# Layer 0's output weights split early, kept in DRAM and loaded ready-made

## The chip, the core and the metric

The kernel runs on one core of a Trainium2 chip. The core has five engines that each take their own instructions strictly in order and meet only at semaphores: TensorE (PE, matrix products and transposes into PSUM), VectorE (DVE), ScalarE (ACT), GpSimd (POOL) and SyncE (SP). In this kernel SP computes nothing; it issues the DMA transfers between DRAM and the on-chip memory SBUF, also in order. The metric is the device time of one execution in microseconds, the median of several runs.

## What is computed

Two encoder layers over 1024 tokens of width 1024. Layer 0 has a banded attention (A), a dense attention (B) and a cross-attention into 256 memory tokens (X); layer 1 has a differential attention and a cross-attention. In both, the heads' outputs are joined, gated and sent through one output matrix `w_out`:

```python
def even_layer(x, mem_n, table, norm_g, w_in, sink, q_norm, k_norm, w_mem_kv, w_out):
    h = rmsnorm(x, norm_g)
    aq, ak, av, bq, bk, bv, xq, gate = _split(h @ w_in, EVEN_SPLITS)
    y_a = windowed_gqa_sink(heads(aq, A_HEADS), heads(ak, A_KV_HEADS), heads(av, A_KV_HEADS), sink, table)
    qb = apply_axial_rope(rmsnorm(heads(bq, B_HEADS), q_norm), cos, sin)
    kb = apply_axial_rope(rmsnorm(heads(bk, B_KV_HEADS), k_norm), cos, sin)
    y_b = dense_gqa_blocked(qb, kb, heads(bv, B_KV_HEADS))
    y_x = memory_cross_attention(heads(xq, X_HEADS), mem_n, w_mem_kv)
    y = jnp.concatenate([y_a, y_b, y_x], axis=-1) * jax.nn.silu(gate)
    return x + y @ w_out
```

The kernel computes float32 products with operands of a reduced format (`fp32r`): each operand is split into a high part, `hi = fp32r(x)`, and a low part, `lo = fp32r(x - hi)`, and a product is the sum of three, hi·hi + hi·lo + lo·hi. So every weight tile needs a cast (the high part) and a subtraction (the low part) before PE can use it.

## The kernel before, in words

**Steps.** The attention of a layer is a list of steps; `run_steps` walks through it. Layer 0 has 8 steps of cross-attention (`NX = 8`), then 8 of the first dense head, then 64 in which dense and banded heads alternate by the string `PAT`. In the iteration of a dense step, PE computes the scores (`sb`, L511); DVE takes their minimum (`mn`), ACT the exponential (`mr` and `e`, L1068), DVE the reciprocal of the sum (`rz`) and POOL multiplies (`e`, L1072). One iteration later SP sends the result through a transfer, `er<-e` (`word_copy`, 512 KB; it copies the words into a tile of the other type). Three iterations after the scores PE transposes it (`te`, L542) in two PSUM banks, and ACT and DVE take the banks apart into `PTh` (L316) and `PTl` (L317). Every second step PE multiplies these with the values (`ob`, L1085). A banded step has the same shape with `sa`, `ta`, `PTa` and `oa`.

**Filling.** Between these, `Jobs` feeds PE with matmuls of other work, 8 at a time: the projections of the layer (`acc<-h,wh` and `acc<-h,wl`, L298) and, at the end of the list, the first part of the output projection (`pre`, L664, jobs made by `pre_jobs`). A projection job's weights are loaded into `wr` (two buffers), and split into `wh` and `wl` by DVE and POOL, when the job before it starts.

**Output weights.** `w_out` of a layer is 1024 x 1024, used as two halves of columns (`nh`) with 8 pieces of 128 rows (`k`) each. Its high and low parts go into tiles with the tag `h`, which hold the layer's normalized input until the last projection job, `last_gates`, has used it; the first half can be filled once that job's first half is done (`half_done`). From then on `wout_hook` calls `load_wout` for one piece at each call, twice in each step: a load of 256 KB into `wor` (a buffer `wr`, or a buffer `sg` for odd pieces), a cast on ACT into `woh` (L258) and a subtraction into `wol` (L259), on DVE for even pieces and on POOL for odd ones. A job `pre` may start when the 8 pieces of its half have been asked for.

**Order.** The program is written step by step, but the order on each engine is made by a scheduler that moves instructions between neighbouring steps by its own estimates. What runs is that order, engine by engine; a DMA, too, waits in SP's order for whatever it needs, with all transfers behind it.

## Time and profile before

| | us |
|---|---|
| median of 3 runs (1239.6 to 1243.0) | 1241.22 |
| the profiled execution's own time | 1242.6 |
| its span in the profile | 1240.8 |

The profile is that of one execution. Its page gives the busy time of each engine, the span in slices, the chain of work that ended last, and groups of like instructions. A row of a group reads: line, engine, operation, out<-in with its shapes, count, then busy time and mean duration of one, then the idle time of the engine in front of it with what ended it. A row of the timeline reads: start, duration, engine, line, operation, operands and count, and in brackets how long the engine stood idle before it and for whom. "issue" there means that the profile shows no one that was waited for. Matmuls overlap, so that the distance of their starts, not their duration, tells the pace.

### The profile page before, as it was taken

The numbers are of one execution on the slowest core, as the hardware profiler recorded it, in microseconds if no ns is written. First come the engines' busy times: TensorE is split into PE (matmuls) and PEld (weight loads), VectorE is DVE, ScalarE is ACT, GpSimd is POOL, SyncE is SP. The second block draws the span as 40 slices with busy tenths as digits, with TensorE's granted clock in tenths as the row PEclk, the third lists the DMA queues.
The fourth block names the chain that finished last, engine by engine and source line by source line (L and its number), as shares of the span: only waits on it lengthen the run. The fifth ranks groups of instructions, "written<-read, shape, count | busy, mean of one in ns | idle before, by whom it ended". The sixth has DMA issues, their size and how long they took to land. (4 is left out here: it accounts for less than half of the span.)

```text
span 1240.8 us, 19673 instructions
## 1 busy us (share of the span) xinstructions
PE 1204.3 (97%) x6806; PEld 1003.4 (81%) x6806; DVE 808.4 (65%) x1479; ACT 651.7 (53%) x1453; POOL 411.3 (33%) x390
## 2 busy tenths in 40 slices
PE   6999999999999999999999999999999999999997
PEld 4788888888887778887888788888787878887886
DVE  5547665477778778647355866766767676668544
ACT  6248754367667766533157733544544454456322
POOL 5023365466666655403122221222222121223100
PEclk9999999999999999999999999999999999999999
DMA  6654445545465565375645333243342432546364
GB/s 255 194 195 146 161 170 165 165 158 202 176 229 200 204 227 196 148 213 193 192 161 157 124 108 120 94 143 102 111 134 77 138 116 102 162 140 204 118 198 146
DMA packets 96638, 199.91 MB, mean 161 GB/s; under 512 B 11510, under 2 KB 31222, under 8 KB 96540
## 3 DMA queue, kind: packets, MB, share of 16 engines
q1 hardware_dynamic: 96540, 198.66, 47.8%
q8 instruction: 54, 0.88, 0.3%
q14 instruction: 44, 0.36, 0.1%
HBM read 79.32 MB, written 31.47 MB: 89 GB/s over the span
## 5 line engine op out<-in xcount | busy, mean ns | idle before, releaser
L298 PE MATMUL acc<-h,wh 128*128 128x512 f32 x1536 | 498.8, 398 | 1.6 <-DVE wh L240 0.6
L298 PEld LDWEIGHTS acc<-h,wh 128*128 128x128 f32 x1536 | 283.0, 188 | 66.3 <-issue 12.2
L298 PE MATMUL acc<-h,wl 128*128 128x512 f32 x768 | 304.7, 397 | 1.6 <-POOL wl L242 1.6
L242 POOL TENSOR_TENSOR wl<-wr,wh 128x512 fp32r<-128x512 f32 x96 | 124.1, 1294 | 335.7 <-DVE wh L240 146.7
L317 DVE TENSOR_TENSOR PTl<-te,PTh 128x512 fp32r<-128x512 f32 x224 | 148.5, 687 | 119.9 <-ACT PTh L316 117.3
L1466 ACT ACTIVATE e<-e,mn 128x1024 f32<-128x1024 f32 x96 | 110.2, 1149 | 125.9 <-DVE mn L1463 125.8
L298 PEld LDWEIGHTS acc<-h,wl 128*128 128x128 f32 x768 | 144.5, 188 | 35.2 <-issue 4.7
L316 ACT CAST PTh<-te 128x512 fp32r<-128x512 f32 x224 | 125.1, 590 | 18.5 <-PE te L542 15.2
L1463 DVE CUSTOM_DVE_ANT_0 e<-sc,toep 128x1024 f32<-128x1024 f32 x96 | 114.0, 1217 | 6.0 <-PE sc L1457 5.8
L1072 POOL TENSOR_TENSOR e<-e,rz 128x1024 f32<-128x1024 f32 x48 | 92.4, 1928 | 74.1 <-DVE rz L1071 56.9
L542 PEld LDWEIGHTS te<-identr,er 128*128 128x128 f32 x896 | 92.1, 143 | 17.5 <-issue 3.7
L542 PE MATMUL te<-identr,er 128*128 128x128 f32 x896 | 99.1, 245 | 4.9 <-issue 2.5
L240 DVE CAST wh<-wr 128x512 fp32r<-128x512 f32 x112 | 58.7, 526 | 38.2 <-PE acc L298 17.8
L1475 DVE SCALAR_TENSOR_TENSOR e<-e,mr 128x1024 f32<-128x1024 f32 x48 | 76.3, 1589 | 1.3
L1490 PE MATMUL oc<-PTh,v 128*128 128x256 f32 x384 | 74.8, 288 | 0.3 <-DVE ckl L1371 0.3
L664 PE MATMUL po<-woh,yh 128*128 128x512 f32 (+1 forms) x172 | 66.3, 385 | 0.0
L664 PE MATMUL po<-woh,yl 128*128 128x512 f32 (+1 forms) x172 | 66.1, 384 | 0.0
L664 PE MATMUL po<-wol,yh 128*128 128x512 f32 (+1 forms) x172 | 66.0, 384 | 0.0
L1063 DVE TENSOR_REDUCE mn<-sb 128x1 f32<-128x1024 f32 x48 | 58.4, 1217 | 7.2 <-PE sb L511 6.7
L1490 PEld LDWEIGHTS oc<-PTh,v 128*128 128x128 f32 x384 | 61.4, 191 | 0.7 <-DVE ckl L1371 0.6
L1068 ACT ACTIVATE e<-sb,mr,nrq 128x1024 f32<-128x1024 f32 x48 | 57.9, 1206 | 1.9
L319 ACT ACTIVATE yh<-yr 128x256 fp32r<-128x256 f32 (+2 forms) x56 | 24.0, 448 | 66.4 <-DMA yr<-ysc 33.8
(199 smaller groups left out, 2256.7 us busy)
## 6 DMA issues: line engine op xcount, KB each, us to landing
er<-e SPq DMA_DIRECT2D x112, 512.0 KB, 3.0
wr<-in_w_in SPq DMA_DIRECT2D x96, 256.0 KB, 2.7
ysc<-gy SPq DMA_DIRECT2D x16, 512.0 KB, 2.6
wor<-in_w_out SPq DMA_DIRECT2D x32, 256.0 KB, 3.3
cq<-sg SPq DMA_DIRECT2D x64, 128.0 KB, 2.9
ck<-sg SPq DMA_DIRECT2D x48, 128.0 KB, 2.3
er<-e SPq DMA_DIRECT2D x12, 384.5 KB, 2.9
xpsc<-xh SPq DMA_DIRECT2D x18, 256.0 KB, 2.4
```

The source lines that it names most:

```text
L240: nc.vector.tensor_copy(hi, raw)
L242: (nc.vector if fast else nc.gpsimd).tensor_tensor(out=lo, in0=raw, in1=hi, op=ALU.subtract)
L298: lastmm[0] = nc.tensor.matmul(acc, a, b[:, k, c0:c0 + n], start=(i == 0), stop=(i == 23))
L316: nc.scalar.copy(hi, src)
L317: return nc.vector.tensor_tensor(out=lo, in0=src, in1=hi, op=ALU.subtract)
L542: nc.tensor.transpose(to[:, i * P:(i + 1) * P], e[0][:, k * P:(k + 1) * P], idt)
L664: lastmm[0] = nc.tensor.matmul(acc, a, b, start=(start and n == 0), stop=(stop and n == 2))
L1072: nc.gpsimd.tensor_tensor(out=et, in0=et, in1=rz.to_broadcast([P, 1024]), op=ALU.mult)
L1463: nc.vector.tensor_tensor_reduce(out=et, in0=Sp, in1=toeps[h][:, w0:w0 + 1024], scale=1.0, scalar=BIG, op0=ALU.add, op1=ALU.min, accum_out ...
L1466: nc.scalar.activation(et, et, AF.Exp, bias=mn[:, m:m + 1], scale=-1.0, accum_out=z[:, m:m + 1])
L1475: nc.vector.scalar_tensor_tensor(out=es[0], in0=es[1], scalar=c, in1=es[0], op0=ALU.mult, op1=ALU.add)
L1490: nc.tensor.matmul(acc, V[:, kt, v, :], pt[:, kt, :], start=(n == 0), stop=(n == 23))
```

## The change

Layer 0's `w_out` is split earlier and in smaller pieces. From the step after the last of the cross-attention and one more (`i > NX`), each iteration of `run_steps` calls `early.step()`, until 32 pieces of 128 x 256 are done: it stores the two parts of the piece before into DRAM (`wo_d`, one tensor for each half and part), loads the next piece into half of a `wr` buffer, casts it on ACT and subtracts on POOL. The two results stand in a new pool `stage` with one buffer for each part.

`load_wout` then loads, for layer 0, the high and the low part from DRAM straight into the tiles `h`, 256 KB each, with no cast and no subtraction. Layer 1 stays as it was. A job `pre` with `k` pieces may now start when `k` pieces of its half have been asked for instead of 8, in both layers.

```diff
+    wo_d = [[[dr.tile([P, 8, 512], F32R, name="wo%d%d%s" % (l, nh, c)) for c in "hl"] for nh in range(2)]
+            for l in range(2)]
...
+    class Early:
+        def __init__(self, l, tiles):
+            self.l, self.n, self.tiles, self.held = l, 0, tiles, None
+
+        def store(self):
+            if self.held is not None:
+                hi, lo, nh, k, c = self.held
+                for d, t in zip(wo_d[self.l][nh], (hi, lo)):
+                    dma(d[:, k, c:c + 256], t)
+                self.held = None
+
+        def step(self):
+            self.store()
+            if self.n < 32:
+                i, c = divmod(self.n, 2)
+                nh, k = divmod(i, 8)
+                c = c * 256
+                self.n += 1
+                raw = wp.tile([P, 512], F32, tag="wr", name="wor", bufs=2)[:, 0:256]
+                dma(raw, w_out[self.l][KORD[self.l][k], :, nh * 512 + c:nh * 512 + c + 256])
+                hi, lo = self.tiles()
+                nc.scalar.copy(hi, raw)
+                nc.gpsimd.tensor_tensor(out=lo, in0=raw, in1=hi, op=ALU.subtract)
+                self.held = hi, lo, nh, k, c
...
     def load_wout(l, i, pl):
...
+        hi, lo = (t[:, k, :] for t in wtile[nh])
+        if l == 0:
+            for t, d in zip((hi, lo), wo_d[l][nh]):
+                dma(t, d[:, k, :])
+            return hi, lo
         raw = sg(M, "wor", F32) if i % 2 else wp.tile([P, 512], F32, tag="wr", name="wor", bufs=2)
         dma(raw, w_out[l][KORD[l][k], :, nh * 512:(nh + 1) * 512])
-        hi, lo = (t[:, k, :] for t in wtile[nh])
-        (nc.vector.tensor_copy if WHI[l] else nc.scalar.copy)(hi, raw)
+        nc.scalar.copy(hi, raw)
...
-                    when=lambda k=k, nhs=nhs: len(wout) >= 8 * nhs[-1] + 8 and all((l, m) in stored for m in range(k))))
+                    when=lambda k=k, nhs=nhs: len(wout) >= 8 * nhs[-1] + k and all((l, m) in stored for m in range(k))))
...
+    stage = pool(left, "stage", "left")
+    early = Early(0, lambda: [stage.tile([P, 256], F32R, tag="wo" + c, name="wo" + c, bufs=1) for c in "hl"])
...
+        if i > NX:
+            early.step()
```

Where instructions move, the scheduler's order shows it. First ACT in the middle of the alternating heads of layer 0 (about 319 us in the profile). Before (`yt` is the evacuation of a head's output, `gy` a gate):

```order
L439 COPY yt<-oa 64x256
L316 CAST PTh<-te 128x4x128 x3
L1067 ACTIVATE mr<-mn,rq 128x1
L316 CAST PTh<-te 128x4x128
L1068 ACTIVATE e,z<-sb,mr,nrq 128x1024
```

and now, where line numbers are those of the changed file (L470 for L439, L347 for L316, L1101 for L1067, L1102 for L1068):

```order
L470 COPY yt<-oa 64x256
L270 CAST woh<-wor 128x256
L347 CAST PTh<-te 128x4x128 x2
L270 CAST woh<-wor 128x256
L347 CAST PTh<-te 128x4x128
L1101 ACTIVATE mr<-mn,rq 128x1
L347 CAST PTh<-te 128x4x128
L1102 ACTIVATE e,z<-sb,mr,nrq 128x1024
```

Two early casts now stand among the casts that feed PE, one of them ahead of a PTh.

Second, SP in the same stretch. Before (`wr` is a projection's weight, `ysc` takes a finished head pair):

```order
L176 DMA er<-e 128x641
L176 DMA ysc_94<-gy 128x1024
L176 DMA wr<-in_w_in 128x512
L176 DMA er<-e 128x769
L176 DMA wr<-in_w_in 128x512
L176 DMA er<-e 128x1024 x2
```

and now (`wo01h` and `wo01l` are the tensors in DRAM for the second half of the columns):

```order
L175 DMA er<-e 128x641
L175 DMA wor<-in_w_out 128x256
L175 DMA er<-e 128x769
L175 DMA wo01h<-woh 128x256
L175 DMA wo01l<-wol 128x256
L175 DMA wor<-in_w_out 128x256
L175 DMA wo01h<-woh 128x256
L175 DMA wo01l<-wol 128x256
L175 DMA wr<-in_w_in 128x512
L175 DMA er<-e 128x1024
```

Loads and stores of the pieces now stand between the `er` transfers.

Third, the place of the output weights themselves (about 380 us): ACT before,

```order
L427 ACTIVATE gy<-acc 128x512
L258 CAST woh<-wor 128x512
L1146 ACTIVATE e,z_4444<-e,mn_4443 128x385
L439 COPY yt<-oa 64x256
L316 CAST PTa<-ta 128x3x128
L316 CAST PTa<-ta 128x2x128
L258 CAST woh<-wor 128x512 x5
L1067 ACTIVATE mr<-mn,rq 128x1
L1068 ACTIVATE e,z<-sb,mr,nrq 128x1024
L439 COPY yt<-oa 64x256
L316 CAST PTh<-te 128x4x128 x2
L258 CAST woh<-wor 128x512 x2
```

where the casts of eight pieces stand between the attention's instructions, and are gone now. What stands there instead is on SP:

```order
L175 DMA er<-e 128x1024 x2
L175 DMA woh<-wo00h 128x512
L175 DMA wol<-wo00l 128x512
L175 DMA woh<-wo00h 128x512
L175 DMA wol<-wo00l 128x512
L175 DMA er<-e 128x641
L175 DMA woh<-wo00h 128x512
L175 DMA wol<-wo00l 128x512
L175 DMA woh<-wo00h 128x512
L175 DMA wol<-wo00l 128x512
L175 DMA woh<-wo00h 128x512
L175 DMA er<-e 128x1024
```

Up to five of the ready-made loads stand ahead of one `er`.

More of the change, by code (lines that the diff above doesn't have):

```diff
@@ L37 @@
 PAT = "BBABBABBABBABBAA" * 4
-WHI = (0, 0)
 WRATE = (1, 2)
```

## The prediction

> **What bounds the kernel now.** I read the page's first lines, then the engines' busy time by stretch, then the rows of TensorE (PE) in order of time for the stretch in which the output weights of layer 0 are made ready.

> ```profile
> span 1240.8 us, 19673 instructions
> PE 1204.3 (97%) x6806; PEld 1003.4 (81%) x6806; DVE 808.4 (65%) x1479; ACT 651.7 (53%) x1453; POOL 411.3 (33%) x390
> ...
> 155.00:340.00 185.00, 184.56 (x1079) 159.09 (x1078) 117.86 (x224) 103.25 (x227) 108.11 (x91) 1.00 0.49 172
> 340.00:372.00 32.00, 32.00 (x199) 27.75 (x199) 25.31 (x51) 21.44 (x53) 20.62 (x21) 1.00 0.67 232
> 372.00:520.00 148.00, 139.29 (x854) 119.38 (x853) 113.46 (x223) 103.35 (x244) 86.14 (x77) 0.97 0.56 196
> ```

> The columns of a stretch are its length, the busy time of PE, PEld, DVE, ACT and POOL, the granted PE clock, the DMA share and GB/s. PE bounds the kernel: it does not do less work after the change, so only its idle time and its slow clock can be won. From 155 to 372 us there is none: PE is busy 184.56 of 185.00 us, then 32.00 of 32.00. From 372 to 520 us, where the 16 pieces of w_out are cast and subtracted, it is idle 148.00 - 139.29 = 8.71 us and its clock falls to 0.97. That is the stretch the change empties; the early stretch is the one it fills.

> **First hole, 389 to 392 us.** Rows of PE, then of DVE and POOL (start, duration, what, and in brackets the idle time before):

> ```profile
> 388.37 0.39 PE L298 MATMUL acc<-h,wl 128*128 128x512 f32 x1
> 388.60 0.39 PE L298 MATMUL acc<-h,wh 128*128 128x512 f32 x1
> ...
> 392.08 0.50 PE L542 MATMUL te<-identr,er 128*128 128x128 f32 x4 [2.51 <-issue]
> ...
> 394.11 0.63 PE L298 MATMUL acc<-h,wh 128*128 128x512 f32 x1
> 394.54 0.63 PE L298 MATMUL acc<-h,wl 128*128 128x512 f32 x1
> ...
> 385.27 4.59 DVE L259 TENSOR_TENSOR wol<-wor,woh 128x512 fp32r<-128x512 f32 x2
> ...
> 391.31 1.27 DVE L317 TENSOR_TENSOR PTl<-te,PTh 128x512 fp32r<-128x512 f32 x2
> ...
> 384.91 3.80 POOL L259 TENSOR_TENSOR wol<-wor,woh 128x512 fp32r<-128x512 f32 x3
> ```

> The transposes at 392.08 need a PSUM bank that PTl of 391.31 empties. That PTl is late because DVE sat in two wol subtractions from 385.27 to 389.86; two of them take 2 x 0.68 = 1.4 us when free. They end just after POOL's three, at 388.71, so DVE stood still while POOL did the same kind of work. After the change neither engine subtracts here. Price of the hole: 2.51 us.

> The hole costs more than itself. 512-column matmuls started every 0.23 us before it (388.37, 388.60) and every 0.43 us after it (394.11, 394.54). Granted clock (first number after the five engines) by pieces of 8 us:

> ```profile
> 388.00:396.00 8.00, 5.49 (x25) 4.42 (x24) 7.36 (x13) 5.36 (x12) 5.26 (x5) 0.83 0.73 233
> 396.00:404.00 8.00, 7.63 (x51) 6.72 (x50) 5.76 (x11) 4.36 (x13) 3.87 (x4) 0.96 0.86 290
> ...
> 420.00:428.00 8.00, 6.18 (x33) 5.27 (x32) 5.91 (x12) 5.15 (x12) 4.71 (x5) 0.79 0.68 224
> ```

> Lost at the first hole: (0.17 + 0.04) x 8 = 1.7 us; at the second 0.21 x 8 = 1.7 us. So holes of about 2 us are worth 1.7 us more than they measure here. [...]

> **Second hole, 422 to 424 us.**

> ```profile
> 418.47 1.07 SPq L176 DMA_DIRECT2D wor<-in_w_out  x2
> ...
> 420.23 0.91 PE L542 MATMUL te<-identr,er 128*128 128x128 f32 x8
> ...
> 422.08 1.26 ACT L258 CAST woh<-wor 128x512 fp32r<-128x512 f32 x2 [1.05 <-DMA wor<-in_w_out]
> ...
> 423.45 0.56 ACT L316 CAST PTh<-te 128x512 fp32r<-128x512 f32 x1
> ...
> 424.06 0.58 PE L1085 MATMUL ob<-PTh,v 128*128 128x256 f32 x1 [1.82 <-ACT PTh L316]
> ```

> The transposes of 420.23 are done by 421.1, but ACT takes its instructions in order, and the woh casts ahead of PTh waited for a transfer issued at 418.47. PTh starts at 423.45 and PE waits 1.82 us for it. With the casts gone from ACT's queue, PTh is bound by the transposes. Price: 1.82 us, and 1.7 us of clock.

> **The change, part by part.**

> ```profile
> L258 ACT CAST woh<-wor x32: 602/621/651, 381.2 to 1131.8; 128x512 fp32r<-128x512 f32 x32
> L259 DVE TENSOR_TENSOR wol<-wor,woh x16: 671/684/3985, 382.0 to 1132.5; 128x512 fp32r<-128x512 f32 x16
> L259 POOL TENSOR_TENSOR wol<-wor,woh x16: 1262/1297/2282, 384.9 to 1126.7; 128x512 fp32r<-128x512 f32 x16
> ...
> L553 ACT CAST sg<-acc 128x256 fp32r<-128x256 f32 x4 | 1.5, 372 | 10.4 <-PE acc L298 6.8 <-DVE lp L1013 3.6
> ...
> L632 POOL TENSOR_TENSOR gy<-yt,gy 128x256 f32<-128x256 f32 x16 | 11.8, 740 | 31.5 <-DVE yt L629 31.4
> ...
> wor<-in_w_out SPq DMA_DIRECT2D x32, 256.0 KB, 3.3
> ...
> bq_d<-sg SPq DMA_DIRECT2D x24, 128.0 KB, 2.1
> aq_d<-sg SPq DMA_DIRECT2D x24, 128.0 KB, 2.4
> ```

> The rows of woh and wol give minimum/median/maximum for both layers; half are layer 0's. *Removed* between 381 and 427 us: 16 casts x 0.62 = 9.9 us of ACT, 8 x 0.68 = 5.4 us of DVE, 8 x 1.30 = 10.4 us of POOL, 16 loads. Only where they stood in front of PE's next operand do they count: the two holes, **-(2.51 + 1.7) - (1.82 + 1.7) = -7.7 us**. What is late next: for the first, the transfer er, some 4 us early by the rows below; for the second, PTh's own transposes. Both leave PE with nothing to wait for.

> *Moved in place of them*: 32 loads of 256 KB (woh and wol ready-made) where 16 stood: 4.2 MB more over some 45 us, about 93 GB/s on a stretch that has 196, where 290 GB/s occurs (396 to 404). On SP up to five of them stand ahead of one er transfer. How much er may be late:

> ```profile
> 336.08 0.47 SPq L176 DMA_DIRECT2D er<-e  x1
> ...
> 343.24 0.84 PE L542 MATMUL te<-identr,er 128*128 128x128 f32 x8
> ```

> er goes out three steps before its transposes: 343.24 - 336.08, less 3.0 us to landing (the page's median for er), leaves 4.2 us. Five loads of 0.26 MB at 290 GB/s are 4.5 us, if er had to stay behind all of them; they are issued over several steps, so I take 0. Bounds: 0 to +3.5 us (one hole like the second). If the cover of 4.2 us is gone, that hole is the cost.

> *Added* between about 155 and 335 us, one piece per step: 32 loads and 64 stores of 128 KB, 32 ACT casts of 128x256 (nearest row 0.372 us: 11.9 us), 32 POOL subtractions of 128x256 (nearest row 0.740 us: 23.7 us). ACT goes from 103.25 to 115 of 185 us, POOL from 108.11 to 132. The work lies beside PE's; the waits are the risk, because a cast waits for its load and, the two staging tiles having one buffer each, for the store of the piece before. Load, cast, store, next cast: the next cast cannot start before 0.37 + 0.4 (issue) + 2.1 to 2.4 (landing of stores of this size) = 2.9 to 3.2 us. A step is about 4.2 us long (the transposes of 330.59 and 343.24 us are three steps apart), so on average it fits. The tightest place in the new order of ACT is a cast, two PTh casts, and the next cast already, ahead of a third PTh. In the trace of before:

> ```profile
> 319.45 1.08 ACT L316 CAST PTh<-te 128x512 fp32r<-128x512 f32 x2
> 321.53 0.59 ACT L316 CAST PTh<-te 128x512 fp32r<-128x512 f32 x1 [1.01 <-PE te L542]
> ...
> 324.48 0.28 PE L1085 MATMUL ob<-PTh,v 128*128 128x256 f32 x1
> 330.59 0.84 PE L542 MATMUL te<-identr,er 128*128 128x128 f32 x8
> ```

> First cast at 319.43, the second not before 322.3 to 322.6, so that PTh moves from 321.53 to about 322.9, mr and the next exponential queue behind it, and PE wants PTh at 324.48: 322.9 + 0.6 still comes before. So the slack of about 2.4 us takes a delay of 1.4 us even there. Bounds for all 32: 0 below (nothing in these rows can make PE faster, it is at 100%), and above, since one of layer 0's 16 casts of before cost PE 3.5 us, 32/16 x 3.5 = 7.0 us. The nearest rows are those of the same stretch, where ACT and POOL already waited often and PE did not; I take **+1.5 us**.

> POOL's subtractions can also hold up DVE's casts wh of the projection weights:

> ```profile
> 324.82 1.89 POOL L1072 TENSOR_TENSOR e<-e,rz 128x1024 f32<-128x1024 f32 x1 [2.76 <-DVE rz L1071]
> 325.00 2.00 DVE L240 CAST wh<-wr 128x512 fp32r<-128x512 f32 x1
> ```

> This cast ended 0.3 us after POOL's instruction did. [...] Bounds: 0 to 32 x 0.74 = 23.7 us of DVE, which has 185 - 117.86 = 67 us to spare, and PE did not wait for this cast of 2.00 us. I take 0.

> SP gets 96 more issues, each past an er; SP waits for others most of that stretch, and a store placed ahead of an er waits for a POOL result that POOL makes before that e. Nothing. The condition for starting output jobs (k pieces instead of 8) lets the first one begin earlier, but it comes behind the last gates in the list of jobs, and the order of PE has it in the same place: 0. In layer 1 the order of PE does not change: 0.

> *Sum*: -4.2 - 3.5 + 1.5 = **-6.2 us** on the profiled execution's 1242.6 us: 1236.4. That execution is 1.4 us above the median of 1241.22, so against the runs shown: **1235.0 us**.

> **Rivals.** The first row is a third hole of the stretch; the others, from the view of the casts' tile, say how long ACT stood for their loads and how often:

> ```profile
> 444.31 0.49 PE L1194 MATMUL oa<-PTa,av 128*128 128x256 f32 x1 [1.95 <-ACT PTa L316]
> ...
> its engine sat idle before it (us, times) until:
>   DMA wor<-in_w_out: 12.0, 9
> ```

> About 0.3%, 3.7 us, is what this measurement can tell from no change: faster is below 1237.5, slower above 1244.9.

> 1. *The casts stop ACT (slower).* Mechanism of the second hole, now at 32 places: a cast waiting for the landing of a store or load stands ahead of PTh or an exponential. Nine of the casts of before waited for their load, 12.0 us together, and one in nine made PE wait. Were each of the 32 to wait and one in nine to reach PE, that is 3.6 holes x 3.5 = 12.5 us, net +4.8: 1246 us. It decides from (7.7 + 3.7)/3.5 = 3.3 holes. For it: one buffer per staging tile. Against: slack of 2.4 us at the tightest place, and most casts stand where ACT was idle. 0.14.
> 2. *Partly given back (same).* Two such holes, or one and a late er: -7.7 + 7 = 1240.5 us. 0.14.
> 3. *The holes only change their cause (the change does not do what it says).* Another hole of this stretch, 1.95 us at 444.31, has nothing to do with w_out, so the stretch has other late operands; if the two holes keep half their size: 1239 us. 0.10.
> 4. *The clock does not come back* (other short waits keep it low): -2.51 - 1.82 + 1.5 = -2.8: 1238.4 us. For it: the clock falls at every hole near 2 us, and any one left keeps its price. 0.06. [...]

> **How the numbers follow.** My forecast has 0.56. Its best case takes the third hole too (1.95 + 1.7, since its cause, an er delayed on POOL, may move) and no early cost: 1241.2 - 7.7 - 3.7 = 1229.8, a little less with the small waits. The upper end is rival 1's 1246. Range 1228.5 to 1246. Faster 0.56; same 0.14 + 0.10 + 0.06 = 0.30; slower 0.14.

> **What would show it.** Right: PE idle from 372 to 520 us falls from 8.7 us to under 4.5 us and no 8 us piece near 390 and 422 has a clock under 0.95; PE stays above 99% from 155 to 340 us; er lands in under 6 us near 385. Wrong: waits of PE for ACT PTh or DVE PTl between 155 and 340 us, with ACT idle for DMA of wor or of the stores; PE waiting for te behind a late er; or new holes after 426 us, where the order of all engines shifts a little.

## The result, and the profile after

The changed kernel takes 1251.88 us (median of 5 runs, 1249.29 to 1252.41); the kernel before, run beside it, 1240.51 us (1239.6 to 1243.0). The ratio is 1.0084 with a 95% interval of 1.0073 to 1.0094: about 10 us slower, where 6.2 us faster was forecast (1235.0 us); it also lies above 1246 us, the upper end of the range. The profiled execution has a span of 1249.7 us.

The page's first lines, and then, by windows, the same stretches of time as were shown of before (length, busy time of PE, PEld, DVE, ACT and POOL, granted clock, DMA share, GB/s):

```profile
span 1249.7 us, 19861 instructions
PE 1204.2 (96%) x6806; PEld 999.6 (80%) x6806; DVE 799.2 (64%) x1471; ACT 654.1 (52%) x1469; POOL 422.3 (34%) x414
```

```profile
155.00:340.00 185.00, 173.30 (x967) 145.15 (x966) 106.06 (x199) 99.70 (x223) 112.58 (x104) 0.99 0.62 205
340.00:372.00 32.00, 31.19 (x192) 27.16 (x192) 22.34 (x47) 21.72 (x55) 22.42 (x22) 0.96 0.71 245
372.00:520.00 148.00, 143.67 (x907) 123.76 (x905) 112.67 (x233) 102.54 (x247) 85.22 (x79) 1.00 0.71 252
```

PE's busy time is the same as before (1204.2 against 1204.3 us), so the span grew by idle time of PE: 8.9 us. From 372 to 520 us idle time fell from 8.71 to 4.33 us and the clock is back at 1.00. That looks like the gain that was forecast, though the same stretch of time no longer holds quite the same work; e1_gain below measures the gain alone. From 155 to 340 us, where PE had been idle for 0.44 us, it is now idle for 11.70 us. DVE too did less there (106.06 instead of 117.86 us): the work of that stretch was pushed back.

PE's rows with the largest holes of that stretch (start, duration, what, in brackets the idle time before and who ended it):

```profile
164.16 1.05 PE L829 MATMUL ssq<-small,sq 128*128 128x2 f32 x8 [2.20 <-ACT sq L816]
...
260.38 0.44 PE L542 MATMUL sa<-ak,q 128*128 128x384 f32 x1 [1.09 <-DVE mn L1176]
...
298.87 1.13 PE L573 MATMUL te<-identr,er 128*128 128x128 f32 x8 [1.07 <-DVE PTl L348]
...
305.44 0.39 PE L1119 MATMUL ob<-PTh,v 128*128 128x256 f32 x1 [1.02 <-ACT PTh L347]
...
325.72 0.79 PE L1228 MATMUL oa<-PTa,av 128*128 128x256 f32 x5 [0.73 <-DVE PTa L348]
...
330.55 1.01 PE L1228 MATMUL oa<-PTa,av 128*128 128x256 f32 x7 [0.57 <-DVE PTa L348]
...
337.71 1.13 PE L573 MATMUL te<-identr,er 128*128 128x128 f32 x8 [2.38 <-DVE PTl L348]
```

They name many different operands. Behind them stand three chains. The first goes through a buffer. Rows of all engines around 325 us:

```profile
321.32 0.38 SPq L175 DMA_DIRECT2D wr<-in_w_in  x1
...
324.06 0.81 DVE L241 CAST wh<-wr 128x512 fp32r<-128x512 f32 x1 [0.78 <-DMA wr<-in_w_in]
...
324.55 0.91 POOL L271 TENSOR_TENSOR wol<-wor,woh 128x256 fp32r<-128x256 f32 x1
...
325.48 0.33 SPq L175 DMA_DIRECT2D wr<-in_w_in  x1
...
328.49 0.43 DVE L241 CAST wh<-wr 128x512 fp32r<-128x512 f32 x1 [2.29 <-DMA wr<-in_w_in]
...
329.48 1.02 DVE L348 TENSOR_TENSOR PTa<-ta,PTa 128x384 fp32r<-128x384 f32 x2
```

A piece of `w_out` holds one of the two buffers `wr` until POOL has subtracted it, at 324.55 + 0.91 = 325.46 us. Only then, at 325.48 us, can SP issue the load of a projection weight into that buffer. DVE takes its instructions in order and waits 2.29 us for it at the cast `wh`; `PTa` is queued behind, and PE waits 0.57 us for that (330.55 us above; 0.73 us at 325.72 us behind the cast of 324.06 us). The group of these casts, in the page of before and then of after, and who waited between 155 and 345 us in the view of waits (us in total, times, longest):

```profile
L240 DVE CAST wh<-wr 128x512 fp32r<-128x512 f32 x112 | 58.7, 526 | 38.2 <-PE acc L298 17.8
```

```profile
L241 DVE CAST wh<-wr 128x512 fp32r<-128x512 f32 x112 | 57.0, 511 | 45.3 <-DMA wr<-in_w_in 20.9
```

```profile
DVE wh L241 <- DMA wr<-in_w_in: 10.4, 8, 2.8
...
ACT woh L270 <- DMA wor<-in_w_out: 13.6, 7, 3.4
ACT woh L270 <- DMA wo00h<-woh: 5.9, 5, 2.2
...
ACT woh L270 <- DMA wo01h<-woh: 3.6, 3, 2.0
...
SPq L175 <- POOL wol L271: 14.7, 17, 2.8
```

Before, DVE's largest wait at these casts was for PE's own results (17.8 us in the whole execution); now it is for transfers of `wr`. Between 155 and 345 us the kernel before shows no wait of `wh` for `wr` at all, the changed one 10.4 us. ACT, too, stands in front of early casts, for their loads (13.6 us) and for the store of the piece before (5.9 + 3.6 = 9.5 us). The wait for the store is the second chain, at 333 to 338 us:

```profile
333.44 0.52 SPq L175 DMA_DIRECT2D wo01h<-woh  x1
...
336.04 0.40 ACT L270 CAST woh<-wor 128x256 fp32r<-128x256 f32 x1 [2.02 <-DMA wo01h<-woh]
336.35 1.06 ACT L347 CAST PTh<-te 128x512 fp32r<-128x512 f32 x2
...
336.96 1.29 DVE L348 TENSOR_TENSOR PTl<-te,PTh 128x512 fp32r<-128x512 f32 x2 [2.48 <-ACT PTh L347]
```

The cast waits 2.02 us for the store that still reads its buffer; `PTh`, `PTl` and PE's transposes (337.71, 2.38 us) follow.

The third chain is shorter: a cast that waits for its own load stands ahead of what PE needs next. Rows in front of the hole at 164.16 us, and then the same cast in e4_nostore (below), which has no stores:

```profile
160.07 0.33 SPq L175 DMA_DIRECT2D wor<-in_w_out  x1
...
162.31 0.41 ACT L270 CAST woh<-wor 128x256 fp32r<-128x256 f32 x1 [1.88 <-POOL e L1106]
...
163.51 0.60 ACT L816 ACTIVATE sq<-acc 128x512 f32<-128x512 f32 x1
```

```profile
162.10 0.40 ACT L268 CAST woh<-wor 128x256 fp32r<-128x256 f32 x1 [1.88 <-DMA wor<-in_w_out]
```

The load goes out at 160.07 us, the cast starts at 162.31 us, and `sq`, for which PE waits 2.20 us, stands behind it. The profile of the changed kernel puts the cast's wait down to POOL's `e`; that of e4_nostore puts an equally long wait down to the load.

Of the holes shown, those at 298.87, 325.72 and 330.55 us (2.37 us together) belong to the first chain, those at 260.38 and 337.71 us (3.47 us) to the second and the one at 164.16 us (2.20 us) to the third. At 305.44 us `PTh` also stands behind an early cast, but the profile does not say what that cast waited for.

Two of these holes also cost PE's clock. Granted clock in the 6 us after four of them:

```profile
164.00:170.00 6.00, 5.84 (x28) 4.80 (x29) 4.35 (x9) 4.59 (x9) 3.46 (x4) 0.72 0.84 309
260.00:266.00 6.00, 5.62 (x36) 5.13 (x37) 5.14 (x13) 3.51 (x10) 4.12 (x3) 1.00 0.81 276
299.00:305.00 6.00, 4.67 (x28) 3.62 (x28) 3.40 (x7) 3.26 (x8) 6.00 (x6) 1.00 0.66 213
338.00:344.00 6.00, 5.94 (x30) 5.09 (x30) 3.94 (x10) 4.57 (x13) 3.13 (x4) 0.72 0.68 229
```

After the holes of 2.20 and 2.38 us it is 0.72, a loss of 0.28 x 6 = 1.7 us each, the price that the forecast had read before; after those of 1.09 and 1.07 us it is 1.00.

### The profile page after: what moved, and what is told of

The parts are those of the page before. It is cut to its first block, busy times and chain, and to the rows that moved or that the text cites. A ratio compares the mean times of both kernels' runs of the same rounds, so it can differ in the third digit from the quotient of the medians.

```text
span 1249.7 us, 19861 instructions
## 1 busy us (share of the span) xinstructions
PE 1204.2 (96%) x6806; PEld 999.6 (80%) x6806; DVE 799.2 (64%) x1471; ACT 654.1 (52%) x1469; POOL 422.3 (34%) x414
## 5 line engine op out<-in xcount | busy, mean ns | idle before, releaser
L329 PEld LDWEIGHTS acc<-h,wh 128*128 128x128 f32 x1536 | 283.6, 189 | 67.9 <-issue 13.2
L347 ACT CAST PTh<-te 128x512 fp32r<-128x512 f32 x224 | 125.2, 590 | 17.9 <-PE te L573 16.8
L1102 ACT ACTIVATE e<-sb,mr,nrq 128x1024 f32<-128x1024 f32 x48 | 57.9, 1207 | 1.7 <-issue 0.4
## 6 DMA issues: line engine op xcount, KB each, us to landing
wr<-in_w_in SPq DMA_DIRECT2D x96, 256.0 KB, 2.8
cq<-sg SPq DMA_DIRECT2D x64, 128.0 KB, 2.6
ck<-sg SPq DMA_DIRECT2D x48, 128.0 KB, 2.3
xpsc<-xh SPq DMA_DIRECT2D x18, 256.0 KB, 2.6
```

Of the source, the lines that this page charges most:

```text
L329: lastmm[0] = nc.tensor.matmul(acc, a, b[:, k, c0:c0 + n], start=(i == 0), stop=(i == 23))
L347: nc.scalar.copy(hi, src)
```

## The experiments

All times are medians; the ratio is to the kernel before, run beside each. "us" is (ratio - 1) x 1240.5, so that runs of different batches can be compared.

| run | what it is | time | ratio (95%) | us |
|---|---|---|---|---|
| changed kernel | | 1251.88 | 1.0084 (1.0073 to 1.0094) | +10.4 |
| e1_gain | no early work | 1232.42 | 0.9931 (0.9914 to 0.9948) | -8.6 |
| e2_cost | early work, cast in place as before | 1260.83 | 1.0148 (1.0120 to 1.0175) | +18.4 |
| e3_noload | no early loads | 1244.88 | 1.0030 (1.0017 to 1.0042) | +3.7 |
| e4_nostore | no early stores | 1244.31 | 1.0023 (1.0009 to 1.0038) | +2.9 |
| e5_inlo | pieces not in `wr` | 1245.51 | 1.0038 (1.0025 to 1.0051) | +4.7 |
| e6_pool | casts on POOL | 1258.01 | 1.0140 (1.0124 to 1.0157) | +17.4 |
| e7_work | no loads, no stores | 1248.42 | 1.0068 (1.0048 to 1.0089) | +8.4 |
| e8_few | 4 of 16 pieces early | 1237.88 | 0.9979 (0.9969 to 0.9990) | -2.6 |
| e9_eight | 8 of 16 pieces early | 1238.18 | 0.9981 (0.9970 to 0.9993) | -2.4 |
| e10_pinned | no loads, no stores, casts pinned | 1238.90 | 0.9979 (0.9966 to 0.9991) | -2.6 |
| e11_sooner | as e5, started sooner | 1256.21 | 1.0119 (1.0096 to 1.0142) | +14.8 |
| e12_dve_two | 2 pieces early, subtractions on DVE | 1234.99 | 0.9958 (0.9945 to 0.9970) | -5.2 |
| e13_dve | before, subtractions on DVE | 1237.68 | 0.9972 (0.9962 to 0.9982) | -3.5 |
| e14_wr | e10 and loads through `wr` | 1245.82 | 1.0041 (1.0028 to 1.0055) | +5.1 |
| e15_store | e10 and stores | 1238.86 | 0.9978 (0.9969 to 0.9987) | -2.7 |
| e16_pinned_all | changed kernel, casts pinned | 1248.66 | 1.0061 (1.0044 to 1.0078) | +7.6 |
| e17_pinned_nostore | e16 without stores | 1243.94 | 1.0026 (1.0015 to 1.0036) | +3.2 |

### Gain and cost apart

e1_gain calls no `early.step()`, and `load_wout` reads parts of the same size elsewhere. e2_cost leaves out the new branch in `load_wout`.

```diff
 # e1_gain
-        if i > NX:
-            early.step()
...
-            for t, d in zip((hi, lo), wo_d[l][nh]):
-                dma(t, d[:, k, :])
+            for n, t in enumerate((hi, lo)):
+                dma(t, bq_d[(2 * i + n) % 6][:, nh * 512:(nh + 1) * 512])
```

> Left out: the early pieces of w_out; the output stage loads ready-made parts of the same size from another tensor in DRAM. So only the gain of the change is left. Forecast's own term: the holes at 389 and 422 us go and nothing is added: 7.7 us under before, about 1233 us; PE idle from 372 to 520 us under 4.5 us, and 0 to 0.5 us from 155 to 340 us. Rival (the gain seen in the changed kernel is a by-product of the early holes, which let the other engines run ahead): within 3 us of before, and PE idle of 7 us or more from 372 to 520 us.

> The early pieces are made and stored, but the output stage casts and subtracts w_out in place as before; the stored parts are not used. So only the cost is left. If cost and gain simply add: the changed kernel plus the 7.7 us of the gain, about 1258 to 1260 us, PE idle about 11.7 us from 155 to 340 us and about 8.7 us from 372 to 520 us. If the early delay also shortens the later holes: 1250 to 1254 us and under 6 us idle from 372 to 520 us.

Two stretches of e1_gain, then of e2_cost:

```profile
155.00:340.00 185.00, 184.56 (x1078) 158.93 (x1078) 117.73 (x223) 103.33 (x226) 108.57 (x90) 1.00 0.49 171
...
372.00:520.00 148.00, 142.91 (x900) 122.59 (x899) 108.60 (x223) 97.85 (x233) 76.10 (x72) 1.00 0.66 234
```

```profile
155.00:340.00 185.00, 173.13 (x966) 145.00 (x966) 106.15 (x199) 99.68 (x222) 112.24 (x104) 0.99 0.61 205
372.00:520.00 148.00, 138.84 (x851) 118.62 (x850) 114.55 (x227) 104.91 (x247) 92.13 (x82) 0.98 0.60 212
```

Without the early work the gain is 8.6 us, with 148.00 - 142.91 = 5.09 us idle left in the later stretch (a little more than the 4.5 us expected) and the clock at 1.00. With the early work alone the loss is 18.4 us, with 11.87 us idle in the early stretch and 9.16 us in the later one. They add: -8.6 + 18.4 = +9.8 us, against +10.4 us. So the gain is the change's own, and the whole miss lies in the early work.

### Leaving out loads or stores

```diff
 # e3_noload
-                raw = wp.tile([P, 512], F32, tag="wr", name="wor", bufs=2)[:, 0:256]
-                dma(raw, w_out[...])
+                raw = hh[:, k, c:c + 256]
 # e4_nostore: no dma in store(), load_wout as in e1_gain
```

> As the changed kernel, but the early pieces are not loaded: cast and subtraction read a tile that is always resident (the stored parts are then of other data); the buffers wr are not touched by the pieces. Theory L (the load: casts on ScalarE, and casts wh on VectorE, stand waiting for transfers of wor and wr that share two buffers): the holes at 164, 299, 302, 305, 318 to 321, 326 and 331 us go, 7.3 us, and about 2 us of slow clock, leaving those at 260 and 338 us (3.5 us): about 1242.5 us. Theory S (the store: one staging buffer, a cast waits for the store of the piece before): within 2 us of the changed kernel, 1250 to 1253 us. [...]

> As the changed kernel, but the early parts are not stored; the output stage loads ready-made parts of the same size from another tensor. Casts wait for their loads and for nothing of the stores. Theory L: only the holes at 260 and 338 us go (3.5 us and up to 1.7 us of clock): 1246 to 1249 us. Theory S: PE idle from 155 to 340 us falls under 3 us: 1236 to 1240 us. [...]

Each gives back about 7 us (6.7 and 7.5), so neither theory L nor theory S holds alone. The reading is limited: without its load or store a cast is free to be placed elsewhere by the scheduler. In e3_noload the casts stand from 25 to 281 us, in the changed kernel from 123.5 to 359.5 us.

### Without the shared buffers, and with the casts on POOL

```diff
 # e5_inlo
-                raw = wp.tile([P, 512], F32, tag="wr", name="wor", bufs=2)[:, 0:256]
+                hi, lo = self.tiles()
+                raw = lo.bitcast(F32)
 # e6_pool
-                nc.scalar.copy(hi, raw)
+                nc.gpsimd.tensor_copy(hi, raw)
```

> As the changed kernel, but each piece is loaded into its own low tile and subtracted there in place: the two buffers wr stay with the projection weights, and a load now waits for the store of the piece before, so that the chain load, cast, subtract, store, load of a piece gets longer (about 6.5 us for a step of 4.2 us). Theory R (the shared wr buffers make the casts wh late): VectorE does not wait for wr any more and the holes behind wh at 299, 326 and 331 us go: 1246 to 1249 us. Theory C (the chain of a piece through one staging buffer is what stops ScalarE and POOL): slower than the changed kernel, 1255 to 1265 us, though no wh waits.

> As the changed kernel, but the 32 early casts stand on POOL, ahead of their subtractions; ScalarE has nothing of the pieces left. If the waits reach PE through ScalarE's order (a cast that waits for its load or for the buffers of the piece before stands ahead of PTh, sq or an exponential): 1240 to 1244 us. If they go over to POOL and reach PE through e, er and its transposes instead: 1250 us or more, and PE waits for te or for VectorE's PTl.

e5_inlo is 5.7 us better than the changed kernel (+4.7 against +10.4) and close to theory R's range: no cast `wh` waits for a transfer of `wr` any more. The 5.7 us need not be the buffers' alone, since the scheduler moved the casts here too (they stand from 32.7 to 384.9 us). Theory C is wrong, although ACT waits as long as in the changed kernel for the loads of the pieces:

```profile
ACT woh L270 <- DMA wol<-in_w_out: 14.0, 9, 3.9
```

e6_pool loses 7.0 us more than the changed kernel: freeing ACT does not help, because the waits go over to POOL, where `wl` and the products `e` of all heads are queued behind them. Between 155 and 345 us POOL stands 9.0 us for loads and 11.5 us for stores in front of the casts, and DVE 19.0 us for `wr`. ACT's order was one way of the delay to PE, not its cause.

### The work alone

e7_work joins the edits of e3_noload and e4_nostore. e10_pinned adds a pin to it:

```diff
-                nc.scalar.copy(hi, raw)
+                with tc.issue_after(lastexp[0].ins):
+                    nc.scalar.copy(hi, raw)
```

`lastexp` is the last exponential written, that of the step before.

> Neither loads nor stores of the early pieces: the cast and the subtraction read a resident tile, and the output stage loads parts of the same size from another tensor. Left are 32 casts on ScalarE and 32 subtractions on POOL through one buffer each. If load and store each cost what their leaving out gave back (7.0 and 7.6 us) and add up: 1251.9 - 14.6 = 1237.3 us, that is 4.9 us above the gain alone. If the order of the engines alone stops them (a cast waits for POOL to read the buffer of the piece before): 1241 to 1245 us, PE idle over 5 us from 155 to 340 us. If only transfers cost: 1232 to 1234 us.

> As e7_work (no loads, no stores, cast and subtraction read a resident tile), but each cast is pinned behind the exponential of the step before on ScalarE, so that the 32 casts stand about where they stand in the changed kernel. It measures the work alone at its place. If transfers make the cost (theories L and S together): 1232 to 1235 us, PE idle under 1.5 us from 155 to 372 us. [...]

e7_work told something else than was asked. The view of its line L268 (minimum, median and maximum in ns, first and last start):

```profile
L268 ACT CAST woh<-h x32: 394/406/423, 24.9 to 73.9; 128x256 fp32r<-128x256 f32 x32
```

With nothing to wait for, the scheduler put all 32 casts between 25 and 74 us, and PE lost its time there (holes of 6.32 us at 57.05 us and of 5.30 us at 71.49 us). In e10_pinned they stand from 147.5 to 343.2 us, near the places of the changed kernel:

```profile
155.00:340.00 185.00, 181.46 (x1043) 154.21 (x1042) 113.89 (x217) 108.79 (x247) 124.83 (x117) 1.00 0.47 167
340.00:372.00 32.00, 31.81 (x201) 27.81 (x201) 24.19 (x49) 22.71 (x56) 22.17 (x21) 1.00 0.64 215
```

The work alone costs 6.0 us (from -8.6 to -2.6), give or take some 2.6 us; PE is idle for 3.73 us in these two rows, and for 0.44 us in e1_gain. So it is not transfers alone, as one theory had it. How much of it is the time on ACT and POOL and how much a delay of DVE beside POOL's subtractions (e8_few below shows one, 3.56 us where 0.68 us is free) was not tried.

### Loads and stores added to the pinned work

e14_wr gives the subtraction of e10_pinned its load back and leaves the cast on resident data; e17_pinned_nostore lets the cast read the load as well; e15_store has stores and no loads; e16_pinned_all is the changed kernel with the pin. Against the changed kernel, beside the pin:

```diff
 # e14_wr; like e17_pinned_nostore, it has no dma in store() and load_wout as in e1_gain
-                nc.scalar.copy(hi, raw)
+                nc.scalar.copy(hi, hh[:, k, c:c + 256])
 # e15_store
-                raw = wp.tile([P, 512], F32, tag="wr", name="wor", bufs=2)[:, 0:256]
-                dma(raw, w_out[...])
+                raw = hh[:, k, c:c + 256]
```

> As e10_pinned, but the pieces are loaded into the shared buffers wr as in the changed kernel and subtracted from there on POOL; the casts on ScalarE read a resident tile and wait for no load; nothing is stored. If the shared buffers and POOL's wait for the load carry the cost of the loads: 1243 to 1247 us, VectorE waits for wr at casts wh and POOL for wor. If only ScalarE's wait for the load does: 1238 to 1240 us.

> As e10_pinned, but both parts are stored as in the changed kernel; nothing is loaded early. It adds the stores alone to the work alone, at the same places. If the wait for the store of the piece before (one staging buffer) is the larger part of the 13.0 us that transfers cost: 1244 to 1250 us. If the loads are: 1239 to 1242 us.

> The changed kernel with one edit: each early cast pinned behind the exponential of the step before, as in e10_pinned, e14_wr and e15_store. Nothing is left out. If the pins themselves change nothing and these runs add up to the changed kernel: 1250 to 1254 us, ratio to before about 1.008. If the pinned places alone make the work cheap: under 1247 us.

> As e16_pinned_all without the stores: loads through wr, the cast waits for its load, nothing is stored. It differs from e14_wr by ScalarE's wait for the load alone. If that wait carries the last 5 us of the cost: 1249 to 1252 us, as e16_pinned_all. If it takes loads and stores together (a cast late by its load makes the store, and so the next cast, late): within 2 us of e14_wr, 1244 to 1248 us.

Waits between 155 and 345 us in e14_wr, then in e15_store:

```profile
DVE wh L241 <- DMA wr<-in_w_in: 13.1, 8, 3.8
```

```profile
ACT woh L270 <- DMA wo00h<-woh: 9.2, 6, 2.9
ACT woh L270 <- DMA wo01h<-woh: 4.0, 6, 2.3
```

In e15_store ACT waits 13.2 us in front of 12 casts, and the kernel is not slower than with the work alone (-2.7 against -2.6 us): these waits lie beside other work. In e14_wr DVE waits for `wr`, and the kernel loses 7.7 us; that ACT's cast waits for the load as well (e17_pinned_nostore) adds nothing that can be told (+3.2 against +5.1 us). The stores cost only with the loads there: 4.4 us from e17 to e16, give or take some 2.5 us. The pins may not be quite neutral: e16 is 2.8 us better than the changed kernel, but the intervals overlap. No run pinned the casts and gave the loads buffers of their own, so that the cost of sharing `wr` is not fully parted from that of the loads themselves.

### Only some pieces, and POOL's part in the first hole

e8_few and e9_eight make only pieces 2, 4, 13, 14, or 1 to 6, 13 and 14, in the low tile as e5_inlo, with load, cast and store in different steps. e11_sooner is e5_inlo with an earlier start. e13_dve and e12_dve_two (with pieces 13 and 14 early) change the engine in `load_wout`.

```diff
 # e8_few (EGAP = 4); e9_eight has other pieces and EGAP = 3, e12_dve_two (13, 14) and 4
+    EP, EGAP = (2, 4, 13, 14), 4
...
+            ph = self.i % EGAP
+            self.i += 1
+            if ph == 0 and self.n < 2 * len(EP):
...
+                dma(lo.bitcast(F32), w_out[...])
...
+            elif ph == 1 and self.cur is not None:
...
+                nc.scalar.copy(hi, raw)
+                nc.gpsimd.tensor_tensor(out=lo, in0=raw, in1=hi, op=ALU.subtract)
+            elif ph == 2 and self.cur is not None:
...
+                    dma(d[:, k, c:c + 256], t)
...
-        if l == 0:
+        if l == 0 and i in EP:
 # e11_sooner
-        if i > NX:
+        if i >= 0:
 # e13_dve, e12_dve_two
-        (nc.gpsimd if i % 2 else nc.vector).tensor_tensor(out=lo, in0=raw, in1=hi, op=ALU.subtract)
+        (nc.gpsimd if i % 2 and l else nc.vector).tensor_tensor(out=lo, in0=raw, in1=hi, op=ALU.subtract)
```

> Of the 16 pieces of 128x512 of w_out only those that stood in front of the two holes (numbers 2, 4, 13 and 14 in order of loading) are made early, in 8 small pieces, one in four steps, with load, cast and store in different steps and without the wr buffers; the other 12 are cast and subtracted in place as before. If a piece costs only where it waits: both holes go and the cost is under 1 us: 1232 to 1234 us. If each small piece costs 0.6 us (19.5 us / 32) wherever it stands: 1237 us. If the holes are not made by these four pieces but by the work of all sixteen: 1237 to 1241 us, with PE idle over 7 us from 372 to 520 us.

> As e8_few, but eight of the sixteen pieces are made early (numbers 1 to 6, 13 and 14), without the wr buffers; the other eight are cast and subtracted in place. In its order on ScalarE all early casts stand in the first two thirds of the stretch. If what is left in e8_few is the rest of the first hole (1.30 us and its slow clock) and a piece before about 250 us costs nothing: 1233 to 1236 us. If each of the 16 small pieces costs 0.4 us (e5_inlo less the gain alone, 13.1 us / 32): 1239 us. If the pieces that are left still make the holes: 1237 to 1239 us with PE idle over 4.5 us from 372 to 520 us.

> As e5_inlo (all 32 pieces, each loaded into its own low tile, no wr), but the pieces may start with the first step, so that about eight more of them stand before 155 us and the last cast stands at about 340 instead of 385 us. If the crowding between 250 and 385 us is what is left of the cost in e5_inlo (13.1 us above the gain alone): 1238 to 1242 us. If a piece costs about 0.4 us wherever it stands: 1244 to 1247 us, with new holes before 155 us.

> The kernel before with one edit: in layer 0 all 16 subtractions stand on VectorE, none on POOL. Nothing is made early. If POOL's three subtractions in a row hold VectorE: the first hole (2.51 us and its slow clock) goes, the second stays: 1236 to 1238 us. If the number of subtractions on VectorE makes it: 1240 to 1244 us.

> Only the two pieces in front of the second hole (numbers 13 and 14) are made early, in 4 small pieces without the wr buffers, which stand before 100 us; the other 14 are cast in place, and in layer 0 all 14 subtractions stand on VectorE, none on POOL. If VectorE stood still in the first hole because POOL ran three subtractions in a row (in e8_few one of 0.68 us took 3.56 us beside them): the hole at 391 us goes, both holes are gone at nearly no cost, 1232 to 1235 us. If it is the number of subtractions on VectorE that makes the hole: it stays, 1237 to 1240 us, with VectorE's PTl late.

In e8_few the second hole went, the first only shrank. Rows of it:

```profile
385.83 3.79 POOL L293 TENSOR_TENSOR wol<-wor,woh 128x512 fp32r<-128x512 f32 x3
386.62 3.56 DVE L293 TENSOR_TENSOR wol<-wor,woh 128x512 fp32r<-128x512 f32 x1 [0.34 <-ACT woh L292]
...
391.22 0.97 PE L576 MATMUL te<-identr,er 128*128 128x128 f32 x6 [1.30 <-DVE PTl L351]
```

One subtraction that DVE does in 0.68 us when free took 3.56 us beside POOL's three, and ended 0.56 us after them (390.18 against 389.62). Now the rows of e13_dve, where POOL does none:

```profile
384.89 2.49 DVE L259 TENSOR_TENSOR wol<-wor,woh 128x512 fp32r<-128x512 f32 x4
...
390.04 0.51 PE L542 MATMUL te<-identr,er 128*128 128x128 f32 x4 [0.85 <-issue]
```

Four on DVE take 2.49 us, where two took 4.59 us before, and PE's hole falls from 2.51 to 0.85 us, with the clock at 1.00 behind it (1.00 from 388 to 396 us, 0.83 before). So the first hole was POOL's doing, not the number of subtractions.

By these rows this place alone gives 1.66 + 1.7 = 3.4 us, and the whole run is 3.5 us faster; that they agree is partly luck. Over the whole stretch of e13_dve PE is idle for 8.55 us, nearly as long as before (8.71 us), because other holes came; what went is the slow clock (1.00, 0.97 before):

```profile
372.00:520.00 148.00, 139.45 (x877) 118.42 (x875) 117.26 (x237) 105.83 (x248) 76.12 (x70) 1.00 0.56 200
440.64 0.44 PE L511 MATMUL sa<-ak,q 128*128 128x384 f32 x1 [2.23 <-DVE mn L1142]
```

By the rows of e8_few one subtraction on DVE lasted 2.88 us longer than when free (3.56 against 0.68 us) and ended after the last of POOL's three; by those of e13_dve, with none on POOL, four took 2.49 us. Through what POOL's subtractions hold DVE up is not shown.

The early stretch of e12_dve_two:

```profile
155.00:340.00 185.00, 184.56 (x1080) 159.10 (x1079) 117.82 (x224) 103.27 (x228) 108.25 (x90) 1.00 0.49 172
```

PE is idle for 0.44 us there, as in the kernel before. The kernel is 5.2 us faster than before, 1234.99 us, at the upper edge of the 1232 to 1235 us expected; of the first hole 0.81 us is left. It beats both kernels, with four small pieces instead of 32. e9_eight did not beat e8_few. In its profiled execution the hole at 391 us is gone, but a new one stands in the early stretch, where PE waits for a load of `q` that SP issued at 242.10 us:

```profile
246.18 0.55 PE L545 MATMUL sa<-ak,q 128*128 128x256 f32 x1 [2.27 <-DMA q<-aq_d]
```

Whether the pieces' transfers made that load late is not shown.

e11_sooner was wrong by the most, 14.8 us slower than before where 1238 to 1242 us or 1244 to 1247 us were expected: pieces placed sooner made new holes before 155 us (2.32 us at 89.28 us for `vraw`) and did not clear those after 250 us. So the cost of a piece depends on where it stands; no price per piece holds.

## Why the prediction was wrong

**The two holes (-7.7 us): right.** e1_gain measures -8.6 us (-10.7 to -6.5). In the changed kernel idle time from 372 to 520 us fell to 4.33 us, under the 4.5 us named (5.09 us in e1_gain, a little over it), and the pieces of 8 us at 388 and 420 us have a clock of 1.00. The reading of the first hole, DVE held by POOL, was shown by e13_dve (2.51 us before, 0.85 us with no subtraction on POOL). That the sum fits is partly luck: in e1_gain the third hole (1.95 us at 444.31 us, with its slow clock) went too, which the forecast had kept for its best case, while PE still waits 0.97 us for `PTh` at 418.48 us and newly 1.07 us for `mn` at 459.71 us. The price of 1.7 us of slow clock came again, 0.28 x 6 us after the holes of 2.20 and 2.38 us, but not behind every hole of that length (last section).

**32 loads instead of 16 (0): right**, as far as it can be seen: e1_gain has them, and its gain is whole. In the changed kernel `er` lands in 3.2 to 5.4 us between 399 and 450 us, where these loads now stand; under 6 us was the sign named.

**The early work (+1.5 us, at most 7.0): the step that failed.** The forecast took the added work to lie beside PE's, with waits that the slack would cover. Its cost is about 19 us (+10.4 less -8.6), and 18.4 us by e2_cost. The durations were about right (0.407 us for a cast, 0.737 us for a subtraction), the waits were not. In the order of the runs: the work alone 6.0 us (e10 less e1), the loads 5.8 us (e17 less e10; 7.7 us by e14), the stores on top of the loads 4.4 us (e16 less e17), the rest 2.8 us (the changed kernel less e16, the pins). Each of these differences is uncertain by 2 to 2.6 us, so that the last is hardly clear of nothing. Three things in the working were at fault:

- *The buffers.* The forecast asked whether POOL's subtractions delay the casts `wh`, and put 0. Its bound of 23.7 us was the author's estimate, 32 times the 0.74 us of a subtraction on POOL; no run measures that delay at the early pieces, and where such a delay was measured, in e8_few, one subtraction on DVE lost 2.88 us beside three on POOL. The forecast did not ask who else uses `wr`, though the diff shows the pieces take `wr`. A projection weight that had been there a job ahead then came late, and DVE's whole queue with it. e14_wr loses 7.7 us with loads through `wr` although no cast on ACT waits for them, and e5_inlo wins 5.7 us back without the sharing: together they make this the largest transfer term, though neither isolates it.
- *The chain of a piece.* 2.9 to 3.2 us from cast to cast, in a step of 4.2 us, left out the load, its turn in SP's order and POOL's turn. The place called the tightest (`yt`, a cast, two `PTh`, a cast) is the second chain above: the first cast stood 2.02 us for a store, and PE lost 2.38 us. SP, put at nothing, waited 14.7 us for POOL's subtractions, with `er` and the next loads behind; what of this reached PE is not shown.
- *The bound.* 7.0 us took the price of the second hole, 3.5 us among 16 casts, for 32. It bounds one mechanism, casts on ACT ahead of `PTh`; the holes shown above come by five operands (`sq`, `mn`, `PTl`, `PTh`, `PTa`).

**The placing of pieces.** "One per step from 155 to 335 us" was nearly so: 123.5 to 359.5 us, three of them before and six after that range.

**The condition with k, and layer 1 (0): right**, in that e1_gain has the new condition and its gain is whole.

**Rivals.** The first, casts that stop ACT, named the right stretch and sign; its 12.5 us of cost were nearest to the 19. Its mechanism is in the rows above (the second and third chain), and so is the sign named for wrong, PE waiting for `PTh` and `PTl` with ACT idle for loads and stores of the pieces. But it is not the whole: stores alone cost nothing (e15_store), the casts' wait for their loads adds nothing to e14_wr, and moving the casts off ACT made it worse (e6_pool). Its "one in nine" also took the waits of both layers; in layer 0 five casts waited for their load, 6.9 us together, and one in five of 32 would have been 6.4 x 3.5 = 22 us. The third, that the holes only change their cause, holds for some of the idle time but not for the time gained, and the fourth, that the clock stays low, is refuted by e1_gain (1.00 from 372 to 520 us). "PE above 99% from 155 to 340 us" was the sign named for right: it is 173.30 / 185 = 94%.

What stays open: how the 6.0 us of the work alone divide between ACT's and POOL's time and a delay of DVE beside POOL's subtractions; what own load buffers at the same places, or a doubled staging buffer, would do; and the pins' 2.8 us.

## What to carry to other kernels

Before work is put "beside" a full engine, list every buffer it borrows and ask who else waits for that buffer: here the loads through two shared buffers cost 5.8 to 7.7 us, as much as all the work added to ScalarE and GpSimd (6.0 us). An engine that is half idle on average need not have free time in a queue that is taken in order (ScalarE was busy for 99.70 of 185.00 us from 155 to 340 us, and behind one early cast that waited 2.02 us PE lost 2.38 us): price a new instruction by what it waits for and who stands behind it. And before removing the work in front of a hole, find which of its neighbours makes the hole: one word (a subtraction on another engine) brought 3.5 us, where 32 early pieces lost 10.

## What the runs showed of the hardware

```profile
391.00:397.00 6.00, 5.61 (x24) 4.50 (x25) 6.00 (x10) 4.37 (x10) 3.56 (x4) 0.72 0.76 266
428.00:434.00 6.00, 5.52 (x35) 4.70 (x35) 5.70 (x9) 3.92 (x10) 2.48 (x4) 1.00 0.67 235
```

Behind 2.17 us (e5_inlo, 331 us) and 2.23 us (e13_dve, 440 us) it stayed at 1.00. Whatever decides this besides the length is not settled here.
